# A hybrid decoder step on one core: a third buffer for the modulation blocks, six raw buffers instead of five for the experts

## The chip, the cores and the metric

The kernel runs on one core of one Trainium2 chip. The metric is the device time of one execution in microseconds (us), given as the median of several runs. Five engines run side by side, each with its own list of instructions, and wait for each other by semaphores: PE (TensorE, matmuls; PEld is its loading of weights, which overlaps PE), DVE (VectorE), ACT (ScalarE), POOL (GpSimd) and SP (SyncE, which here only issues transfers from HBM).

## The reference

One step of a decoder with two layers for 264 tokens (256 of a prompt, 8 that are decoded), width D = 1024, fp32:

```python
def _layer(x, c, l, p, st):
    mod = jax.nn.silu(c) @ p['w_ada'][l] + p['b_ada'][l]
    sh1, sc1, gt1, sh2, sc2, gt2 = [m[:, None, :] for m in jnp.split(mod, 6, axis=-1)]
    h = x * (1.0 + sc1) + sh1
    m, new_st = _mixer(h, l, p, st)
    x = _layernorm(ALPHA * x + (1.0 + gt1) * m, p['ln_mix_g'][l], p['ln_mix_b'][l])
    h = x * (1.0 + sc2) + sh2
    ...
    if l % 2 == 0:
        f = _swiglu(h, wg, wu, wd)            # layer 0, dense
    else:
        f = _moe(h, router, wg, wu, wd)       # layer 1, 2 of 8 experts
    return _layernorm(ALPHA * x + (1.0 + gt2) * f, p['ln_ffn_g'][l], p['ln_ffn_b'][l]), new_st
```

`_mixer` projects h once with `w_in`, runs three groups of heads on the parts (SSD, a chunked scan; RWKV-7, a recurrence for each token; GLA, a chunked scan), and projects their outputs with `w_out`. The modulation `mod` has 6 x 1024 columns a layer, so `w_ada` is 24 MB a layer, for 9 rows of c: much to load, little to multiply.

## The kernel before

Weights come as blocks of 128 x 1024 fp32 (512 KB). A block of `w_in`, `w_out`, of the dense feed-forward or of an expert goes through `block()`: SP loads it into a raw buffer `w` (L398), ACT copies it to a high part `wh` (L297), DVE subtracts to get a low part `wl` (L318), and PE multiplies it in three fp32r matmuls (hi x hi, hi x lo, lo x hi, L337). A raw buffer is free when DVE has made `wl`.

A block of `w_ada` goes through `ada()`. Its first blocks (tiles `k`, L474) are loaded at the start. The other 80 (tiles `wa`, L477) come in 20 steps of four, spread over both layers by a table (`FILL`) and where a value is needed (`need`). PE multiplies a `wa` block as it is, by the tile `sc` (silu of c): eight matmuls a block, 32 for a step, into the PSUM tile `ada`. A `wa` buffer is free when PE has done its eight matmuls. Then ACT copies `ada` (`adae`) and PE transposes it (`adat`).

Buffers stand in pools with a fixed number of slots. `self.wp` has `NW['w']` slots of 512 KB for raw `w` blocks, `self.ap` has `NW['a']` for `wa` blocks. An expert's block may be at home in either: the string `MOE['wa']` is gone through block by block, a letter for each, and "a" means `self.ap`. The small tiles of the mixers are in pools `f2` (of 128 x 2 x 264) and `f1` (of 128 x 264), numbered by `N2` and `N1`: pool 'r' holds the RWKV stream's tiles (and in the first stage the tiles `k`), pool 't' of `N1` small ones such as `w`, `ed`, `rs8`, `cslot`.

The order of the instructions on each engine is not written out: a list scheduler takes them by priority and by when a slot comes free, so that a changed number of slots also changes the order. All loads of weights and of the decoder's states stand on one queue, SP's, in one order: a load that waits for its slot holds up every load behind it.

```python
        spare = home == "a"
        w = (self.ap if spare else self.wp).tile([128, 1024], F32, tag="wa" if spare else "w", name=f"w_{self.n}")
        self.nc.sync.dma_start(w[:, :n], src)
        ...
                        w = self.ap.tile([128, 4, 256], F32, tag="wa", name=f"wa_{self.n}")
                        self.nc.sync.dma_start(w, src)
        ...
        homes = MOE["wa"]
        ...
            return self.block(self.I["moe"][e, m, b], by="wmoe", home=homes[self.blocks % len(homes)])
```

Names used below: `pj` is a matmul of the projection by `w_in` (from `hh`, `hl`, the two parts of h), `sro` and `gm` small matmuls of the decoder's RWKV read and of a norm, `mu` and `e` the sums of a norm, `gr` a product of the RWKV chunk's keys, `bk` and `sd` tiles that ACT makes for RWKV and for SSD (from `cu`, which is read back from HBM), `eg` the experts' gate and up products, `ed` their down products, `sc` the scattering of an expert's result to its tokens, `x` the residual that takes it, `xg` the gathering of an expert's tokens.

Of the kernel before, what the change touches and what calls it, by code (L numbers as in the profile page):

```python
# [166 lines left out]
def _unpack(r):  # L167
# [26 lines left out]
TP = {'a': 'ada adat st',  # L194
 'd': 'pj op eg0 ed eg1 ssq pos lg',
 'r': 'gr pa pb z p1 p2 p3 pn pr ph pg pc po gm gv gb gg1 ht cs sc gso fd gpo gpk lo gpv xg fg sro gvb pbt'}
N2 = {'r': 11, 'd': 16, 's': 14, 'g': 4, 'a': 1, 'q': 4, 'm': 3}
N1 = {'r': 10, 'd': 2, 's': 8, 't': 13, 'u': 6}
ORDER = [['rwkv', 'conv', 'rstep', 'qkv', 'aff', 'sstep', 'rout', 'gstep', 'gla', 'ssd', 'z2', 'gread', 'z1', 'z0'],
 ['rstep', 'rwkv', 'conv', 'sstep', 'qkv', 'rout', 'gstep', 'aff', 'gla', 'ssd', 'z0', 'z1', 'z2', 'gread']]  # L200
X = {'FR': 1, 'AHEAD': 1, 'SA': 4}
MOE = {'s0': 28, 'ss': 6, 'g0': 31, 'gs': 5, 'wa': 'wawaw', 'e0': 11, 'es': 5}
LOW = {'rout.0': -9440,
 'win.1': -20,
 'sstep.0': -1560,
# [44 lines left out]
 '1.o5': 1,  # L250
 '0.ssd': 1,
 '1.o6': 1}
NW = {'w': 3, 'a': 2, 'h': 3, 'l': 3}
NP = {'a': 1, 'd': 2, 'r': 3, 's': 2}


# [10 lines left out]
class Net:  # L267
    def __init__(self, nc, tc, I, O, stack):
        self.nc, self.tc, self.I, self.O = nc, tc, I, O
        p = lambda name, bufs, **k: stack.enter_context(tc.tile_pool(name=name, bufs=bufs, **k))  # L270
        self.cp = p("const", 1)
        self.wp = p("wts", NW["w"])
        self.ap = p("wada", NW["a"])
        self.hp = p("whi", NW["h"])
        self.lp = p("wlo", NW["l"])
        self.bp = p("big", 1)
        self.p2 = {t: p("f2" + t, n) for t, n in N2.items()}
        self.p1 = {t: p("f1" + t, n) for t, n in N1.items()}
        self.dp = p("scr", 1, space=bass.MemoryType.DRAM)
# [1297 lines left out]
    def experts(self, l, r, last, first=()):  # L1577

        nc, io = self.nc, self.C("iota")
        toks, mask, comb, pos, hth, htl = self.routed  # L1580
        homes = MOE["wa"]

# [10 lines left out]
        def gather(pr):  # L1593

            sel = []
            for t, (t0, n) in enumerate(toks):
                s = self.f1("sel", [128, 2, 128], F32R)
                if t == 2:
                    nc.gpsimd.memset(s.bitcast(F32), 0.0)
                for i in range(2):  # L1600
                    e = 2 * pr + i
                    chosen = self.ts(s[:n, i], io[:n], pos[:n, t, e:e + 1], OP.is_equal, mask[:n, t, e:e + 1], OP.mult)
                sel.append(s)
            yield
            name = "xg" if pr % 2 else "xo"
            xg = [[self.f2(name, [128, 2, 256], F32R) for _ in range(4)] for _ in range(2)]
            for k in range(8):
                for x, src in zip(xg, (hth, htl)):
                    ps = self.ps("xg", [128, 256])
                    for t, (t0, n) in enumerate(toks):  # L1610
                        self.mm(ps, src[t, k // 4][:, k % 4], sel[t].rearrange("p a b -> p (a b)"), t == 0, t == 2)
                    done = self.act(x[k // 2][:, k % 2], ps)
                yield
            self.affine((chosen, done))
            pc = self.ps("cs", [128, 2])
            cslot = self.f1("cslot", [128, 2])
            selt = []
            for i in range(2):
                e = 2 * pr + i
                for t, (t0, n) in enumerate(toks):  # L1620
                    self.mm(pc[:, i:i + 1], sel[t][:n, i].bitcast(F32), comb[:n, t, e:e + 1], t == 0, t == 2)
                ps = self.ps("st")[:, :TT]
                for t, (t0, n) in enumerate(toks):
                    self.tr(ps[:, t0:t0 + n], sel[t][:n, i].bitcast(F32))
                s = self.f1("selt", [128, TT], F32R)
                self.act(s, ps)
                selt.append(s)
            self.act(cslot, pc)
            G[pr] = xg, selt, cslot
            yield  # L1630
# [43 lines left out]
        def scatter(pr):  # L1674
            selt = G[pr][1]
            if last and pr == 3:
                V["st"] = self.stats()
            st = V["st"]
            self.need(l, 5)
            for d in range(8):  # L1680
                ps = self.ps("sc")[:, :TT]
                todo = [(y[:, d % 4], selt[i]) for i, yh, yl in Y[pr, d // 4] for y in (yh, yl)]
                for j, (y, s) in enumerate(todo):
                    self.mm(ps, y, s, j == 0, j == 3)
                self.residual(l, 5, d, ps, st, last=st is not None)
                yield
# [8 lines left out]
        for pr in range(4):  # L1695
            ahead = gather(pr + 1) if pr < 3 else iter(())
            V["at"], V["side"] = 0, [(MOE["s0"], MOE["ss"], back), (MOE["g0"], MOE["gs"], ahead)]
            if pr < 3:
# [4 lines left out]
            else:  # L1703
                for i in range(2):
                    up(pr, i)
                for n in range(2):
                    for i in range(2):
                        down(pr, i, n)
                    if n == 0:
                        for _ in back:  # L1710
                            pass
                        back = scatter(pr)
                        V["side"] = [(V["at"] + MOE["e0"], MOE["es"], back)]
                break
# [43 lines left out]
```

## Time and profile before

| | |
|---|---|
| median of 3 runs | 1104.17 us (1101.29 to 1107.13) |
| profiled execution | 1099.37 us, its span 1097.6 us |
| mean granted clock of TensorE | 0.966 |
| PE busy | 1006.8 us (92%) |
| DVE busy | 741.3 us (68%) |
| ACT busy | 609.6 us (56%) |
| moved by DMA | 238.55 MB, 217 GB/s in the mean |

The order of the stages in the profiled execution, by the timeline: the first modulation blocks and the projection of layer 0 up to some 81 us, the mixer of layer 0 to some 290, the dense feed-forward to some 493, the mixer of layer 1 to some 735, routing, the experts from 756 to 1080, and the end. The share of PE differs between them: in the feed-forward and in the experts it is nearly always busy, in the mixers not.

### The profile page before, as it was taken

How to read it: one execution, taken by the hardware profiler on the slowest of the kernel's cores; microseconds unless marked ns; L12 is line 12 of the kernel's file. 1: busy time of each engine (PE TensorE's matmuls, PEld its weight loads, DVE VectorE, ACT ScalarE, POOL GpSimd, SP SyncE). 2: the span in 40 equal slices, each digit the busy share in tenths (PEclk: the TensorE clock that was granted, in tenths of full speed). 3: DMA queues.
4: the chain of work that ended last, by engine and by line, in shares of the span. 5: the costliest groups of instructions: out<-in, count | busy, mean ns of one | idle time of the engine just before them, and what ended most of it. 6: DMA issues, size and time to landing. Idle time of an engine off the chain costs nothing. (4 is left out here: it accounts for less than half of the span.)

```text
span 1097.6 us, 22445 instructions
## 1 busy us (share of the span) xinstructions
PE 1006.8 (92%) x8944; PEld 825.8 (75%) x8944; DVE 741.3 (68%) x1406; ACT 609.6 (56%) x1037; POOL 87.6 (8%) x191
## 2 busy tenths in 40 slices
PE   6889987889899999998899998979999999999994
PEld 2668765557799999986677876757788888888872
DVE  1567647655765555448786686557879888888884
ACT  2656323543554444337671436438777777777773
POOL 1021222000100000001330220010000000000000
PEclk9999999999899999998989998989999999999998
DMA  9774478854565665555684284332998988898881
GB/s 353 279 216 130 141 206 305 269 179 137 176 207 175 183 181 173 146 162 192 196 253 143 81 275 163 103 101 77 328 323 299 329 321 299 308 327 299 318 299 42
DMA packets 71184, 238.55 MB, mean 217 GB/s; under 512 B 9280, under 2 KB 10016, under 8 KB 71072
## 3 DMA queue, kind: packets, MB, share of 16 engines
q1 hardware_dynamic: 66512, 226.18, 61.9%
q0 software_dynamic: 4000, 10.71, 3.5%
q8 instruction: 72, 1.18, 0.4%
q14 instruction: 40, 0.33, 0.1%
q10 hardware_dynamic: 560, 0.15, 0.1%
HBM read 231.50 MB, written 5.51 MB: 216 GB/s over the span
## 5 line engine op out<-in xcount | busy, mean ns | idle before, releaser
L318 DVE TENSOR_TENSOR wl<-w,wh 128x1024 fp32r<-128x1024 f32 (+1 forms) x324 | 390.1, 1216 | 130.0 <-ACT wh L297 125.8
L297 ACT ACTIVATE wh<-w 128x1024 fp32r<-128x1024 f32 (+1 forms) x324 | 338.4, 1053 | 237.6 <-issue 76.4
L337 PE MATMUL pj<-hh,wh 128*128 128x264 f32 x384 | 120.1, 315 | 6.7 <-ACT cv L297 2.8
L337 PE MATMUL pj<-hl,wh 128*128 128x264 f32 x384 | 120.1, 314 | 0.4 <-DVE hl L318 0.4
L337 PE MATMUL pj<-hh,wl 128*128 128x264 f32 x384 | 118.3, 309 | 1.1 <-DVE wl L318 1.1
L337 PEld LDWEIGHTS pj<-hh,wh 128*128 128x128 f32 x384 | 77.7, 203 | 15.7 <-issue 4.7
L337 PEld LDWEIGHTS pj<-hl,wh 128*128 128x128 f32 x384 | 77.3, 202 | 9.0 <-issue 6.5
L337 PEld LDWEIGHTS pj<-hh,wl 128*128 128x128 f32 x384 | 77.2, 202 | 7.6 <-issue 3.4
L337 PE MATMUL eg<-wh,xg 128*128 128x512 f32 x256 | 81.6, 397 | 0.0
L337 PE MATMUL eg<-wh,xo 128*128 128x512 f32 x256 | 81.5, 396 | 0.0
L337 PE MATMUL ada<-wa,sc 128*32 128x256 f32 x640 | 53.2, 415 | 25.4 <-DMA wa<-in_wada 20.9
L337 PEld LDWEIGHTS eg<-wh,xg 128*128 128x128 f32 x256 | 48.2, 188 | 9.5 <-ACT wh L297 0.3
L337 PEld LDWEIGHTS eg<-wh,xo 128*128 128x128 f32 x256 | 48.1, 188 | 9.2
L337 PE MATMUL eg<-wl,xg 128*128 128x512 f32 x128 | 51.6, 403 | 0.8 <-DVE wl L318 0.8
L337 PE MATMUL ed<-wl,ath 128*128 128x512 f32 x128 | 51.7, 404 | 0.6 <-DVE wl L318 0.6
L337 PE MATMUL eg<-wl,xo 128*128 128x512 f32 x128 | 51.4, 402 | 0.3 <-DVE wl L318 0.3
L337 PE MATMUL fg<-hh,wh 128*128 128x264 f32 x176 | 50.9, 289 | 0.0
L337 PE MATMUL ed<-wh,ath 128*128 128x512 f32 x128 | 50.8, 397 | 0.0
L337 PE MATMUL ed<-wh,atl 128*128 128x512 f32 x128 | 50.5, 395 | 0.0
L337 PE MATMUL fg<-hh,wl 128*128 128x264 f32 x176 | 50.4, 287 | 0.0
L337 PE MATMUL fu<-hh,wh 128*128 128x264 f32 x176 | 50.3, 286 | 0.0
L337 PE MATMUL fg<-hl,wh 128*128 128x264 f32 x176 | 50.2, 286 | 0.0
(486 smaller groups left out, 2282.6 us busy)
## 6 DMA issues: line engine op xcount, KB each, us to landing
w<-in_moe SPq DMA_DIRECT2D x192, 512.0 KB, 4.8
wa<-in_wada SPq DMA_DIRECT2D x80, 512.0 KB, 4.6
w<-in_win SPq DMA_DIRECT2D x48, 512.0 KB, 4.8
w<-in_ffgu SPq DMA_DIRECT2D x44, 512.0 KB, 3.6
k<-in_wada SPq DMA_DIRECT2D x32, 256.0 KB, 5.8
w<-in_wout SPq DMA_DIRECT2D x16, 512.0 KB, 4.5
w<-in_ffd SPq DMA_DIRECT2D x16, 512.0 KB, 3.5
w<-in_ffd SPq DMA_DIRECT2D x8, 384.0 KB, 3.9
```

What stands on the lines that cost most here:

```text
L297: r = self.nc.scalar.activation(out, in_, func, bias=bias, scale=scale)
L318: return (e or self.nc.vector).tensor_tensor(out, a, b, op=op)
L337: return self.nc.tensor.matmul(out, lhsT, rhs, start=start, stop=stop)
```

## The change

Four numbers and a string: `self.ap` gets three slots instead of two; the experts' blocks alternate between three `w` and three `wa` buffers, where before they took three of `w` and two of `wa` in a cycle of five; the pool of RWKV tiles of `f2` has 9 slots instead of 11, that of `f1` 7 instead of 10, and the pool of small tiles 10 instead of 13. The tables of priorities and of fillers stay.

```diff
-N2 = {'r': 11, 'd': 16, 's': 14, 'g': 4, 'a': 1, 'q': 4, 'm': 3}
-N1 = {'r': 10, 'd': 2, 's': 8, 't': 13, 'u': 6}
+N2 = {'r': 9, 'd': 16, 's': 14, 'g': 4, 'a': 1, 'q': 4, 'm': 3}
+N1 = {'r': 7, 'd': 2, 's': 8, 't': 10, 'u': 6}
...
-MOE = {'s0': 28, 'ss': 6, 'g0': 31, 'gs': 5, 'wa': 'wawaw', 'e0': 11, 'es': 5}
+MOE = {'s0': 28, 'ss': 6, 'g0': 31, 'gs': 5, 'wa': 'wa', 'e0': 11, 'es': 5}
...
-NW = {'w': 3, 'a': 2, 'h': 3, 'l': 3}
+NW = {'w': 3, 'a': 3, 'h': 3, 'l': 3}
```

The order of the instructions changes with it nearly everywhere in the mixers and in the experts. Three places follow; in them a number behind a name tells tiles of one name apart.

**PE, one modulation step in the mixer of layer 0** (step `ada_1995`, its four blocks `wa_1996`, `wa_2002`, `wa_2008` and `wa_2014`, with projection matmuls `pj` between). Before, the first two blocks stand together, and what follows up to the third is 20 rows of `sro`, `gm` and `pj`:

```order
L337 MATMUL pj_2068<-hh_347,wh_2064 128x264
L337 MATMUL ada_1995<-wa_1996,sc 32x256 x4
L337 MATMUL ada_1995<-wa_2002,sc 32x256 x4
L337 MATMUL sro_1912<-r_467,srw_1897 64x1 x16
L337 MATMUL pj_2068<-hl_348,wh_2064 128x264
L337 MATMUL pj_2068<-hh_347,wl_2065 128x264
L337 MATMUL pj_2068<-hh_347,wh_2064 128x264
L337 MATMUL gm_2267<-o_589,cst 128x264
```

In the changed kernel three blocks stand together, and the fourth comes after ten rows of `pj`:

```order
L337 MATMUL ada_1995<-wa_2002,sc 32x256 x4
L337 MATMUL ada_1995<-wa_2008,sc 32x256 x4
L337 MATMUL pj_2868<-hh_356,wl_2865 128x264
L337 MATMUL pj_2036<-hh_347,wl_2033 128x264
L337 MATMUL pj_2036<-hh_356,wh_2032 128x264
L337 MATMUL pj_2036<-hl_357,wh_2032 128x264
L337 MATMUL pj_2036<-hh_356,wl_2033 128x264
L337 MATMUL pj_2036<-hh_356,wh_2032 128x264
L337 MATMUL pj_2036<-hl_357,wh_2032 128x264
L337 MATMUL pj_2036<-hh_356,wl_2033 128x264
L337 MATMUL pj_2900<-hh_245,wh_2896 128x264
L337 MATMUL pj_2900<-hl_246,wh_2896 128x264
```

The row behind the last one shown is the block `wa_2014`. The third block moved up to the first two, into the new slot; the fourth is the one that waits for a slot of this step, that of `wa_1996`. Steps before a norm are the exception: there PE still has two blocks, the norm's `mu` and `e`, and two blocks.

**SP, the same stage** (`wa` are modulation blocks; `w_3060` is a block of `w_in`, `w_3143` and `w_3180` are blocks of `w_out`, `sgl` a state of the decoder). Before, loads of the two kinds take turns:

```order
L477 DMA wa_2107<-in_wada 128x1024
L477 DMA wa_2113<-in_wada 128x1024
L477 DMA wa_2129<-in_wada 128x1024
L398 DMA w_3060<-in_win 128x1024
L477 DMA wa_2135<-in_wada 128x1024
L398 DMA w_3143<-in_wout 128x1024
L477 DMA wa_2141<-in_wada 128x1024
L477 DMA wa_2147<-in_wada 128x1024
L1220 DMA sgl_2297<-in_s_gla 128x512
```

In the changed kernel the `wa` loads stand in a run, sixteen of them from `wa_2113` to `wa_2840` with the state `sgl` among them, and the `w` blocks come behind it:

```order
L477 DMA wa_2249<-in_wada 128x1024
L1220 DMA sgl_2297<-in_s_gla 128x512
L477 DMA wa_2701<-in_wada 128x1024
L477 DMA wa_2707<-in_wada 128x1024
L477 DMA wa_2713<-in_wada 128x1024
L477 DMA wa_2719<-in_wada 128x1024
L477 DMA wa_2828<-in_wada 128x1024
L477 DMA wa_2834<-in_wada 128x1024
L477 DMA wa_2840<-in_wada 128x1024
L398 DMA w_3060<-in_win 128x1024
L398 DMA w_3143<-in_wout 128x1024
```

So `w_3060` moved behind fourteen modulation blocks that it stood ahead of.

**PE, in the experts** (each scattering tile `sc` takes four matmuls, and each is followed by additions to `x` on DVE). Before, the four of one tile stand alone among the `eg` products:

```order
L337 MATMUL eg_1704_11751<-wh_11778,xg_11436 128x512
L337 MATMUL sc_12143<-selt_10896,eyh_11177 128x264
L337 MATMUL sc_12143<-selt_10896,eyl_11178 128x264
L337 MATMUL sc_12143<-selt_10905,eyh_11568 128x264
L337 MATMUL sc_12143<-selt_10905,eyl_11569 128x264
L337 MATMUL eg_1704_11751<-wl_11779,xg_11436 128x512
```

In the changed kernel four such tiles stand together behind the last product of an `eg` tile; the first ten rows of it:

```order
L337 MATMUL eg_1723_11910<-wh_11949,xg_11441 128x512
L337 MATMUL sc_12143<-selt_10896,eyh_11177 128x264
L337 MATMUL sc_12143<-selt_10896,eyl_11178 128x264
L337 MATMUL sc_12143<-selt_10905,eyh_11568 128x264
L337 MATMUL sc_12143<-selt_10905,eyl_11569 128x264
L337 MATMUL sc_12237<-selt_10896,eyh_11177 128x264
L337 MATMUL sc_12237<-selt_10896,eyl_11178 128x264
L337 MATMUL sc_12237<-selt_10905,eyh_11568 128x264
L337 MATMUL sc_12237<-selt_10905,eyl_11569 128x264
L337 MATMUL sc_12315<-selt_10896,eyh_11177 128x264
```

The scattering, gathering and sums beside the experts' products stand in 81 pieces instead of 117; nine of them instead of five have more than 0.9 us of PE work. On ACT, where `sd` stood ahead of `bk` in the mixer of layer 0, the first `bk` now stands ahead of `sd`, and the second `bk` and a tile `vt` behind it.

## Rows read from the trace of the kernel before

**Rows 1.** The page: the span, and the engines' busy time.

```profile
span 1097.6 us, 22445 instructions
...
PE 1006.8 (92%) x8944; PEld 825.8 (75%) x8944; DVE 741.3 (68%) x1406; ACT 609.6 (56%) x1037; POOL 87.6 (8%) x191
```

**Rows 2.** Busy time by stretch: the start, layer 0's mixer and its worst part, experts.

```profile
core 0: us, PE busy (x) PEld busy (x) DVE busy (x) ACT busy (x) POOL busy (x), PEclk, DMA share, GB/s
0.00:27.00 27.00, 17.10 (x116) 6.28 (x116) 4.66 (x13) 6.59 (x10) 4.08 (x18) 0.94 0.96 353
135.00:243.00 108.00, 88.21 (x1233) 62.77 (x1234) 64.28 (x157) 40.55 (x92) 16.06 (x27) 0.97 0.76 244
162.00:189.00 27.00, 20.18 (x163) 15.43 (x163) 18.60 (x40) 10.76 (x20) 4.30 (x8) 0.97 0.91 320
756.00:1080.00 324.00, 322.05 (x1563) 261.49 (x1562) 273.63 (x344) 242.08 (x306) 0.62 (x2) 1.00 0.85 299
```

**Rows 3.** Waits, whole span: engine, line, waited for, us, times, longest.

```profile
PEld ada L337 <- DMA wa<-in_wada: 26.3, 23, 3.8
PE ada L337 <- DMA wa<-in_wada: 20.9, 19, 3.6
```

**Rows 4.** The tile `wa`: its loads, and their time from issue to landing.

```profile
L477 SPq DMA_DIRECT2D wa<-in_wada x80: 327/328/839, 30.2 to 683.0; - x80
...
DMA to landing us min/median/max: 3.5/4.6/9.2
```

**Rows 5.** The wait of SP's queue ahead of `wa` loads.

```profile
SPq L477 <- PE ada L337: 116.7, 55, 18.4
```

**Rows 6.** Timeline of PE, 281 to 290 us: start, length, what, [idle before].

```profile
281.34 1.07 PE L337 MATMUL ada<-wa,sc 128*32 128x256 f32 x16
282.34 0.71 PE L337 MATMUL mu<-x,onem 128*128 128x264 f32 x2
282.89 0.62 PE L337 MATMUL e<-sq,onem 128*128 128x264 f32 x2
286.43 1.05 PE L337 MATMUL ada<-wa,sc 128*32 128x256 f32 x8 [2.92 <-DMA wa<-in_wada]
287.70 1.08 PE L337 MATMUL ada<-wa,sc 128*32 128x256 f32 x8 [0.22 <-DMA wa<-in_wada]
```

**Rows 7.** Timeline of SP's queue in the same stretch.

```profile
282.04 0.80 SPq L477 DMA_DIRECT2D wa<-in_wada  x2
```

**Rows 8.** Timeline of PE around 150 and around 186 us.

```profile
150.02 1.08 PE L337 MATMUL ada<-wa,sc 128*32 128x256 f32 x8 [3.57 <-DMA wa<-in_wada]
...
186.26 0.64 PE L337 MATMUL ada<-wa,sc 128*32 128x256 f32 x8 [2.86 <-DVE sst L318]
```

**Rows 9.** Stretches behind two waits for `wa`, columns as in Rows 2.

```profile
149.99:153.40 3.41, 3.38 (x19) 2.57 (x20) 1.50 (x3) 0.60 (x1) 0.56 (x1) 0.50 0.84 267
498.15:504.98 6.83, 6.20 (x35) 4.52 (x36) 6.79 (x21) 5.31 (x14) 2.94 (x9) 0.50 0.77 271
```

**Rows 10.** Timeline of PE, 76 to 84 us, in the mixer of layer 0.

```profile
81.08 0.45 PE L337 MATMUL gr<-sg,ka 64*64 64x64 f32 x12 [4.26 <-ACT bk L297]
```

**Rows 11.** Timeline of ACT in the same stretch.

```profile
78.13 1.27 ACT L297 ACTIVATE sd<-cu,tt 128x128 f32<-128x128 f32 x4 [5.38 <-DMA cu<-ssdd]
```

**Rows 12.** Waits within the experts, 756 to 1080 us.

```profile
ACT wh L297 <- DMA w<-in_moe: 15.5, 26, 1.8
...
PE eg L337 <- DVE wl L318: 1.1, 2, 0.8
...
PE ed L337 <- DVE wl L318: 0.6, 1, 0.6
```

**Rows 13.** Groups of instructions by form, 756 to 1080 us: count, busy, mean ns.

```profile
L318 DVE TENSOR_TENSOR wl<-w,wh 128x1024 fp32r<-128x1024 f32 x189 | 227.2, 1221 | 35.6 <-ACT wh L297 32.6 <-PE ed L337 1.0 <-PE eg L337 0.9
...
L297 ACT ACTIVATE wh<-w 128x1024 fp32r<-128x1024 f32 x189 | 197.3, 1057 | 40.7 <-DMA w<-in_moe 15.5 <-PE eg L337 12.9 <-PE ed L337 8.5
...
L334 DVE SCALAR_TENSOR_TENSOR x<-sc,mod,x 128x256 f32<-128x256 f32 x32 | 15.2, 475 | 0.0
```

## The prediction

> **What bounds the kernel now.** I read the page first, then busy time by stretch, then the waits, then timelines around single waits. The page shows PE busy for 1006.8 of 1097.6 us [rows 1]: 91 us in which it is not are all that better ordering can win. They are not spread evenly. In the experts PE works 322.05 of 324 us, at full clock [rows 2]; there only 2 us are left. In 135 to 243 us, the mixer of layer 0, it works 88.21 of 108 us, and its worst quarter, from 162 to 189, has 20.18 of 27. The list of waits names the largest single cause by PE's own matmuls: 20.9 us in 19 waits for a modulation block, 3.6 us at most [rows 3]. Weight loads wait 26.3 us for the same blocks; the two overlap, so I count the 20.9 and not the sum.
>
> Why is a block late? All 80 loads take 4.6 us from issue to landing at the median, 3.5 at least, 9.2 at most [rows 4]. SP waits 55 times for PE to free one of the two slots [rows 5]: it would load earlier if it could. The timeline at 281 us shows the pattern whole. PE runs two blocks in 1.07 us and has 1.3 us of other work; SP issues the next two at 282.04 when the first slot is free [rows 7], and PE takes the first of them at 286.43, after 2.92 us idle, and the second after 0.22 more [rows 6]. At 150.02 it waits 3.57 us; at 186.26 it waits 2.86 us, which the view puts down to DVE's `sst`, though these matmuls read only `wa` and `sc` [rows 8], so I count it to the block too.
>
> A wait also costs something behind it. From 149.99 the granted clock is 0.50 (1.2 GHz) for 3.41 us, and from 498.15 for 6.83 us, each right behind an idle PE [rows 9]. A stretch of 3.41 us at half clock does 1.7 us of full-speed work, so it costs about 1.7 us.
>
> **The third slot.** For each block I counted the PE work that stands between the block whose slot it takes and the block itself: each instruction in PE's order at the mean spacing that its tile shows in the trace of before, waits left out. A block then waits for what its landing exceeds that work. With a landing of 4.4 us, between the minimum and the median of [rows 4] and chosen because it fits, the two-slot order gives 21.6 us over 19 blocks, where the trace has 20.9 over 19 [rows 3]. That fit is one to the total, not to each block. The changed order with three slots gives 7.4 us over 9 blocks at the same landing. Gain: 14.2 us. At 3.5 us it is 10.2 against 3.3, gain 6.9; at 5.0 it is 35.4 against 15.6, gain 19.8.
>
> What remains follows from the order shown above. Three blocks of a step are now at hand, the fourth takes the slot of the first, and has two blocks and ten `pj` before it: at the spacings counted, about 3 us against 4.4. The steps in front of a norm hardly gain: with two blocks, `mu` and `e` between a slot's release and its next block there are 2.1 us of work, so about 2.3 us of the 2.92 + 0.22 of [rows 6] remain.
>
> **Loads that now go three at a time.** The count takes the same landing for all. Where three slots come free within some 1.1 us (the time of two blocks in [rows 6]) three loads share the transfer engines. At the 320 GB/s of 162 to 189 us [rows 2] 512 KB take 1.6 us, so the third may land up to 1.6 us later than the second. Below, this costs nothing: the third is often the one that is needed last. Above, I take a landing of 5.0 for the new order alone: 15.6 instead of 7.4 us, 8.2 more. I take 2, near the lower end, because the DMA share of the stage is 0.76 [rows 2], and a block loaded ahead of its need can land late for nothing.
>
> The Trainium skill's "DMA: Bandwidth & Descriptors", section "Issuing engines are not separate DMA queues", has the rule that speaks against the change: all transfers run on the same 16 engines and interleave. By it, one more transfer under way is no more bandwidth; taken alone it would put the slots and the clock at nothing and leave 1099.4 + 2 + 4.8 = 1106 us. The trace agrees in so far as the landings reach 9.2 us at a DMA share up to 0.91; it is the first two rivals below.
>
> **The clock.** The drops at 149.99 and behind 186.26 follow waits that the count removes: 2 x 1.7 = 3.4 us. Below, nothing, if a shorter wait there still brings one; above, also the two of 6.83 us behind 286.43 and 498.06, together 10.2 us. I take 3.4, since those two stand at norms, where the wait remains.
>
> **Six raw buffers for the experts.** ACT waits 15.5 us for their blocks, but PE only 1.1 + 0.6 us for what is made of them [rows 12]: the rest is covered by blocks already split. The gain lies between 0 and 1.7 us; I take 0.
>
> **The pieces between the experts' products.** Their PE work is the same. A tile `sc` brings two additions to `x` of 475 ns on DVE, where a `wl` takes 1.22 us [rows 13], and four tiles together hold DVE for some 3.8 us. DVE is busy 273.63 of 324 us [rows 2], so a late `wl` is caught up slowly. Before, five pieces above 0.9 us of PE work went with 1.7 us of PE waiting for `wl` in all [rows 12], 0.34 each. Nine would cost 3.1, or 1.4 more; at the worst each costs 1 us, 9 in all. I take 2, a little above the 1.4 for the busy DVE.
>
> **What else moves.** In the mixer PE waits 4.26 us at 81.08 for `bk` [rows 10], because `sd` ahead of it on ACT waits 5.38 us for `cu` [rows 11]. Now the first `bk` is ahead of `sd` and the second, with `vt`, behind it: PE goes on sooner and stops at the next tile instead. I take 0, with 4.3 us the other way as the bound of a gain, and as much of a loss if both stop. `w_3060`, now behind the run of modulation loads, has 8.9 us of counted PE work between its issue and its use, and needs about 4.6 [rows 4] + 1.06 + 1.22 us [rows 13] = 6.9. I take 0; if the run is issued 5 us late, it costs 3. Fewer slots in pool 'r': in the tiles' lifetimes I find nine of `f2` and seven of `f1` needed at once, so 0. The start, whose `k` tiles use these slots, is held by transfers (share 0.96 [rows 2]), so 0, 1 us at most.
>
> **Sum.** -14.2 - 3.4 + 2 + 2 = -13.6 us. From the profiled execution's 1099.4 that is 1085.8. The median of the runs shown is 4.8 us above that execution, so the forecast is 1091 us.
>
> **Rivals.**
> 1. *The transfers stretch.* If three in flight raise the mean landing of the new order to about 5.2 us, its sum (15.6 at 5.0, 37.4 at 6.0) comes to the 20.9 of now, and nothing is won: 1098 to 1107. For it: a share of 0.91 at 162 to 189 us, landings up to 9.2. Against it: the bytes are the same, and a quarter of the stage's transfer time is free.
> 2. *The same, further, and slower.* At a landing of 6.0 the new order waits 37.4 us, 16.5 more than now: 1104 + 16.5 = 1121. It ends above +0.5% from a landing of about 5.5 on (26.5 us). Its place is 135 to 243 us, where a run of `wa` loads competes with `w` and states. Against it: only the maximum landings are of that size now.
> 3. *The gain comes, and is given back.* PE waits for `w_3060` and the two `w_out` blocks behind it (3 us each, 9), or the experts' pieces cost 9 instead of 2. That leaves 1091 + 7 to 9 = about 1099, with both some 1107. For it: DVE at 84% in the experts. Against it: 322.05 of 324 us busy in spite of pieces of that size.
>
> **How the numbers follow.** What this kernel's measurement can tell from no change is about 0.5%, 5.5 us: 1098.7 to 1109.7. The forecast has 0.54 and a range of its own of 1083 to 1097 (counting at 5.0 in both orders, -19.8, or without the gain of the clock). Rival 1 has 0.15, rival 2 0.11, rival 3 0.20, half of it still below 1098.7. Faster: 0.54 + 0.10 + a little of rival 1 = 0.65; same: 0.22; slower: 0.13. The range that leaves out 2 in 10 is 1081 to 1106.
>
> **What would show it.** Right: PE's waits for `wa` at 7 to 11 us in some ten places, most of them for the fourth block of a step; PE busy for over 88% of the mixer of layer 0, where it is 82% now [rows 2]; granted clock full at 150 and 187; the experts' stretch within 3 us of now. Landing at 4.4 to 5.0 at the median. Wrong by rivals 1 and 2: a median landing above 5.2 and waits of 20 us or more. Wrong by rival 3: new PE waits for DVE `wl`, under `pj` and `op` in the mixer, or under `eg` and `ed` in the experts.

## The result, and the profile after

The changed kernel has a median of 1087.66 us (1085.42 to 1093.90, 4 runs) where the kernel before, beside it, has 1104.14 (1101.29 to 1107.13, 4 runs): a ratio of 0.9876, 95% interval 0.9846 to 0.9906. The forecast was 1091 us, with 1081 to 1106. A second comparison, with more runs on another occasion (run 5 below), gives 1093.57 against 1104.28: 0.9889, 0.9857 to 0.9921. That ratio leaves out three of the changed kernel's twelve executions, those more than 1.5% above its fastest; with all twelve the medians stand at 0.9903. So the change brings some 11 to 16 us. Between the two profiled executions the difference is 12.0 us: the changed kernel's has a span of 1085.6 us, that of [rows 1] 1097.6.

The page of the changed kernel, the span and the engines' busy time:

```profile
span 1085.6 us, 22435 instructions
...
PE 1009.1 (93%) x8944; PEld 825.7 (76%) x8944; DVE 744.1 (69%) x1406; ACT 610.3 (56%) x1037; POOL 85.3 (8%) x191
```

PE's busy time hardly moved; what fell is the time in which it waits. The waits of the whole span that answer to [rows 3] (engine, line, what for, total, times, longest), and with them the wait for the modulation step before, which [rows 3] did not need:

```profile
PEld ada L337 <- DMA wa<-in_wada: 13.9, 10, 2.9
PE ada L337 <- DMA wa<-in_wada: 11.1, 10, 2.4
...
PEld ada L337 <- DVE mod L493: 6.2, 7, 2.7
PE ada L337 <- DVE mod L493: 4.8, 4, 2.5
```

The last of them reads, in the kernel before:

```profile
PE ada L337 <- DVE mod L493: 1.2, 3, 0.4
```

From 20.9 us in 19 waits to 11.1 in 10: half of the places are gone. All ten that are left stand ahead of the fourth block of a step, as the prediction said of most of them; before, eight stood ahead of the third and nine ahead of the fourth. In exchange `ada` now waits for `mod`, 4.8 us instead of 1.2: a step's blocks are at hand, but the one PSUM tile that `ada` shares with `adat` still holds the step before, until DVE has read it. The queue that answers to [rows 5], and the landings that answer to [rows 4]:

```profile
SPq L477 <- PE ada L337: 83.6, 39, 9.4
```

```profile
DMA to landing us min/median/max: 3.4/5.1/9.8
```

Loads wait for PE 39 times, not 55. They take longer, 5.1 us at the median instead of 4.6. Yet the ten blocks that PE waited for landed after 4.7 us in the mean (counted as in the view, one by one: 3.7, 4.2, 6.5, 5.1, 5.7, 5.3, 4.1, 4.4, 4.1, 4.1), the other seventy after 5.6. Before it was the other way round: 5.6 us for the nineteen, 4.8 for the others. The long landings now fall on blocks that were loaded ahead of their need.

Busy time by stretch, layer 0's mixer (as in [rows 2]) and a part of it:

```profile
135.00:243.00 108.00, 95.71 (x1248) 66.10 (x1247) 68.90 (x166) 46.15 (x101) 13.05 (x22) 0.92 0.81 269
188.33:201.98 13.65, 13.55 (x244) 7.86 (x245) 5.33 (x21) 2.55 (x6) 0.00 (x0) 0.50 0.73 218
```

PE is busy for 95.71 of 108 us where it was 88.21, at a higher DMA share. But the granted clock of the row is 0.92 where [rows 2] has 0.97, so some 5 of the 7.5 us (0.05 of 108) can be the same work done more slowly, and the prediction's sign of over 88% is met in part by that. The second row is what was not expected: 13.65 us at half clock with PE busy nearly throughout. Three single waits on the timeline of PE:

```profile
173.42 0.64 PE L337 MATMUL ada<-wa,sc 128*32 128x256 f32 x8 [1.49 <-DVE mod L493]
...
188.43 1.08 PE L337 MATMUL ada<-wa,sc 128*32 128x256 f32 x8 [1.60 <-DMA wa<-in_wada]
```

```profile
278.11 0.64 PE L337 MATMUL ada<-wa,sc 128*32 128x256 f32 x8 [2.11 <-DMA wa<-in_wada]
```

The first is the new wait; the second ends where the half clock begins; the third is the fourth block at the norm, which had 2.92 + 0.22 us in [rows 6].

In the experts the time was not won. Stage lengths, read from the first or last row of a tile on PE's timeline (in brackets the time of it at granted clock 0.50):

| kernel (profiled execution) | 81 us to first `fg` | last `fd` to first `lg` | first `eg` to last `ed` | last `ed` to first `cnt` |
|---|---|---|---|---|
| before | 209.3 (17.4) | 243.0 (33.0) | 318.1 (0) | 11.1 (0) |
| changed | 199.2 (17.1) | 237.6 (27.5) | 317.1 (0) | 15.2 (0) |
| run 1, smaller pools alone | 208.2 (20.5) | 245.9 (36.2) | 318.1 (0) | 11.1 (0) |
| run 2, three slots, old cycle | 204.4 (23.5) | 239.1 (29.3) | 325.7 (0) | 15.2 (0) |
| run 3, scattering earlier | 199.2 (13.7) | 235.0 (18.2) | 323.6 (0) | 10.1 (0) |
| run 4, four slots | 202.4 (31.5) | 243.8 (36.0) | 318.7 (0) | 15.2 (0) |
| run 5, the change again (a long execution, 1101.8 us) | 208.6 (31.1) | 241.2 (35.2) | 317.3 (0) | 15.2 (0) |
| run 6, sums in a row | 195.9 (10.2) | 232.6 (21.4) | 317.8 (0) | 11.0 (0) |
| run 7, four slots, sums in a row | 199.1 (35.3) | 232.5 (11.7) | 319.4 (0) | 11.0 (0) |
| run 8, before with sums in a row | 205.4 (20.1) | 239.4 (31.3) | 320.6 (0) | 9.4 (0) |
| run 11, run 7 again | 195.8 (27.6) | 238.0 (34.2) | 319.4 (0) | 11.0 (0) |

In the first two rows the mixers gave 10.1 and 5.4 us, the experts' products 1.0; the tail behind the last product took 4.1 back. The lengths of the mixers hold the clock of their execution: in run 5 the same kernel has 66.3 us of them at half clock and hardly shorter mixers than before. With half of the time at half clock taken off, both mixers together are 427.1 and 425.8 us with two slots (before, run 1) and 414.5 and 416.6 with the change (changed, run 5), so 9 to 13 us shorter. In the tail PE is not idle. Its timeline in the kernel before, from the last product on:

```profile
1073.08 0.40 PE L337 MATMUL ed<-wh,atl 128*128 128x512 f32 x1
1073.41 0.41 PE L337 MATMUL ms<-x,onem 128*32 128x264 f32 x1
1073.42 0.41 PE L337 MATMUL ms<-sq,onem 128*32 128x264 f32 x1
1073.42 0.41 PE L337 MATMUL ms<-x,onem 128*32 128x264 f32 x1
1073.43 0.41 PE L337 MATMUL ms<-sq,onem 128*32 128x264 f32 x1
...
1074.12 0.39 PE L337 MATMUL ms<-x,onem 128*32 128x264 f32 x1
1074.43 0.39 PE L337 MATMUL sc<-selt,eyh 128*128 128x264 f32 x1
```

and in the changed kernel:

```profile
1057.26 0.40 PE L337 MATMUL ed<-wh,atl 128*128 128x512 f32 x1
1057.49 0.28 PE L337 MATMUL sc<-selt,eyl 128*128 128x264 f32 x1
...
1058.96 0.28 PE L337 MATMUL sc<-selt,eyl 128*128 128x264 f32 x1
1059.29 0.63 PE L337 MATMUL ms<-x,onem 128*32 128x264 f32 x2
1059.75 0.63 PE L337 MATMUL ms<-sq,onem 128*32 128x264 f32 x2
```

`ms` are the sums of the last norm, in four groups of 32 columns. Before, the products of four groups start within 0.02 us of each other, and 14 recorded rows take 1.1 us. Now they come mostly one group at a time, in pieces between `sc` rows: four rows take 1.1 us. Also 29 `sc` rows stand behind the last `ed` and not 16; the other thirteen stood between the products before, so their time, some 1.6 us, only changed its place.

### The profile page after: what moved, and what is told of

It reads as the page before. It is cut to its first block, busy times and chain, and to the rows that moved or that the text cites. A ratio compares the mean times of both kernels' runs of the same rounds, so it can differ in the third digit from the quotient of the medians.

```text
span 1085.6 us, 22435 instructions
## 1 busy us (share of the span) xinstructions
PE 1009.1 (93%) x8944; PEld 825.7 (76%) x8944; DVE 744.1 (69%) x1406; ACT 610.3 (56%) x1037; POOL 85.3 (8%) x191
## 5 line engine op out<-in xcount | busy, mean ns | idle before, releaser
L337 PE MATMUL pj<-hl,wh 128*128 128x264 f32 x384 | 116.4, 304 | 0.2 <-DVE hl L318 0.2
L337 PEld LDWEIGHTS pj<-hh,wl 128*128 128x128 f32 x384 | 76.8, 200 | 10.1 <-issue 6.8
L337 PE MATMUL ada<-wa,sc 128*32 128x256 f32 x640 | 50.9, 412 | 15.1 <-DMA wa<-in_wada 11.1
L337 PE MATMUL fu<-hl,wh 128*128 128x264 f32 x176 | 50.5, 287 | 0.0
```

The lines of the kernel that those rows point to most:

```text
L337: return self.nc.tensor.matmul(out, lhsT, rhs, start=start, stop=stop)
```

## The experiments

All are timed beside the kernel before. "Changed" is the kernel of this study; where a run starts from it, the diff is against it.

**1. The smaller pools alone** (from changed: the third slot and the cycle taken back).

```diff
-MOE = {..., 'wa': 'wa', 'e0': 11, 'es': 5}
+MOE = {..., 'wa': 'wawaw', 'e0': 11, 'es': 5}
-NW = {'w': 3, 'a': 3, 'h': 3, 'l': 3}
+NW = {'w': 3, 'a': 2, 'h': 3, 'l': 3}
```

> The smaller pools of RWKV tiles and small tiles alone, with two buffers for modulation blocks and the experts' five raw buffers as before. The order of every engine is then that of the kernel before, row for row; only addresses move. My theory (the cut slots were never needed together): no change, 1104 us within 3, waits of PE for modulation blocks about 21 us again. Rival (the cut slots cost something that the third buffer hid): 2 us or more above the kernel before.

1104.56 us, ratio 1.0013 (0.9979 to 1.0046). Block waits:

```profile
PE ada L337 <- DMA wa<-in_wada: 23.5, 21, 3.1
```

The cut slots cost nothing, as the prediction had it.

**2. Three slots, the experts' old cycle** (from changed).

```diff
-MOE = {..., 'wa': 'wa', 'e0': 11, 'es': 5}
+MOE = {..., 'wa': 'wawaw', 'e0': 11, 'es': 5}
```

> The changed kernel with the experts' cycle of three w and two wa letters put back (so the third wa buffer is there, and the experts still use all six buffers, in another cycle). My theory (the gain is the modulation blocks'): as the changed kernel, 1088 us within 2, PE's waits for modulation blocks about 11 us, and the stretch from the first eg product to the end as long as in the changed kernel, 332 us, with some 29 scattering matmuls behind the last ed product. Rival (the even cycle of the experts' buffers carries part of the gain, or made the end longer): 3 us or more of difference, in the experts' stretch.

1103.42 us, ratio 1.0016 (0.9978 to 1.0054): the theory missed, and the rival came. Block waits are down as they should be (11.9 us in 10), and the mixers are shorter. But the experts' products take 325.7 us instead of 317.1. Waits of this kernel from 748 to 1074 us:

```profile
ACT wh L297 <- DMA w<-in_moe: 14.2, 27, 2.4
PEld eg L337 <- DVE wl L318: 8.9, 17, 1.1
...
PE eg L337 <- DVE wl L318: 3.6, 8, 0.8
```

and of the changed kernel from 740 to 1058, where no wait of ACT for an expert's block is listed:

```profile
PEld ed L337 <- DVE wl L318: 1.1, 4, 0.3
...
PEld eg L337 <- DVE wl L318: 0.7, 3, 0.3
```

In the kernel before, from 756 to 1080 us, the second line is

```profile
PEld eg L337 <- DVE wl L318: 3.7, 10, 1.1
```

With three slots the scheduler orders the experts as it does in the changed kernel (81 pieces of side work). In the old cycle a `w` buffer comes round after five blocks, in the even cycle over six buffers after six. ACT's wait for raw blocks is no longer here than in the kernel before (15.5 us, [rows 12]), but what follows from it reaches PE: its loading of weights waits 8.9 us for `wl`, with the old order 3.7, with the even cycle 0.7. That the new order, with fewer and larger pieces between the products, leaves less of a reserve of split blocks would fit this; it is not shown by itself.

**3. The last scattering earlier** (from changed).

```diff
-MOE = {..., 'wa': 'wa', 'e0': 11, 'es': 5}
+MOE = {..., 'wa': 'wa', 'e0': 0, 'es': 2}
```

> The changed kernel, with the last pair's first four scattering tiles put between its last four ed blocks in the program (the start of the side work 0 and its step 2 instead of 11 and 5), so that 16 instead of 29 scattering matmuls stand behind the last ed product. Theory: the experts gave back 3 us in the tail behind the last product (10.8 us instead of 6.7 in the kernel before), not in the larger pieces of side work; the tail falls to 6 to 7.5 us and the time by 3 to 4, to 1084. Rival (the pieces cost it, between the products): the tail shortens but the products end as much later, or nothing changes: 1087 to 1089.

1095.46 us, 0.9938 (0.9903 to 0.9972), no gain over the changed kernel. The tail fell from 15.2 to 10.1 us, but the products take 6.5 longer: the rival, though its 1087 to 1089 us were too low as well. `sc` and single `ms` rows now stand between `ed` rows and cost PE the same there. So it is their spacing on PE, not where they stand, that must be paid for; run 6 follows from it.

**4. Four slots** (from changed).

```diff
-NW = {'w': 3, 'a': 3, 'h': 3, 'l': 3}
+NW = {'w': 3, 'a': 4, 'h': 3, 'l': 3}
```

> The changed kernel with a fourth buffer for modulation blocks. My theory (a wait is the landing less the work between a slot's release and its use): the count at a landing of 4.4 gives 0.1 us instead of 7.4, at 5.0 it is 0.8 instead of 15.6, so PE's waits for modulation blocks fall from 11 us to under 3, and the time by 5 to 10, to 1078 to 1083; what is left before a step's first block is the wait for the step before it (one PSUM tile), 4 to 7 us. Rival (transfers bind: four in flight only land later): landings above 6 us at the median, waits of 8 us or more, 1086 to 1092.

1095.97 us, 0.9936 (0.9903 to 0.9968). Its waits, its landings, and a stretch of the mixer:

```profile
PE ada L337 <- DVE mod L493: 5.1, 3, 4.3
...
PE ada L337 <- DVE mod L318: 2.3, 1, 2.3
...
PE ada L337 <- DMA wa<-in_wada: 1.8, 3, 0.9
```

```profile
DMA to landing us min/median/max: 3.4/6.1/12.1
```

```profile
190.47:214.36 23.89, 22.72 (x398) 15.00 (x398) 10.01 (x36) 10.78 (x30) 0.57 (x1) 0.50 0.67 215
```

The count was about right (0.1 to 0.8 us counted, 1.8 measured), at a landing of 6.1 us, so transfers do not bind. The time did not follow: 31.5 and 36.0 us of the two mixers are at half clock, against 17.1 and 27.5, and `mod` is waited for. The mean granted clock over the runs is 0.959, against 0.966 for the changed kernel in run 5. So taking 9 us more of block waits away brought no time in the median.

**5. The change again**, unaltered.

> The changed kernel once more, unaltered, beside the kernel before on one chip in many runs. Three slots, four slots and two slots have shown, in single profiles corrected by half of the time at half clock, 712, 707 and 722 us up to the experts' first product. Theory (the third slot is worth about 10 us ahead of the experts, the experts give back 3): 7 to 9 us below the kernel before at equal granted clock, so 1093 to 1096 where that has 1102.6; PE's waits for modulation blocks 11 to 13 us; experts from the first eg product to the end 332 us. Rival (the gain of 16 us of the first comparison is of the change alone): 1086 to 1088.

1093.57 us, 0.9889 (0.9857 to 0.9921): as expected, and with the first comparison's interval overlapping. In its profile the block waits are 9.9 us in 9 places, a little below what was expected, and the wait for `mod` is 8.5 us in 4. The mean granted clock is 0.966 over 12 runs, for the kernel before 0.960 over 17. At a span near 1100 us the time that the clock takes is at most span x (1 - clock), 37 against 44 us. So up to some 6 of the 10.7 us are the clock's.

**6. The norms' sums in a row** (from changed; in all four norms).

```diff
-                for i, a in zip((0, 64, 32, 96), st["todo"]):
-                    self.mm(st["ms"][i:i + 32, :TT], self.onem[:, :32], a, start=d == 1, stop=d == 5)
+                last = None
+                for i, a in list(zip((0, 64, 32, 96), st["todo"]))[::-1]:
+                    self.tc.cur_priority -= 10 ** 5 if last else 0
+                    r = self.mm(st["ms"][i:i + 32, :TT], self.onem[:, :32], a, start=d == 1, stop=d == 5)
+                    self.tc.cur_priority += 10 ** 5 if last else 0
+                    if last:
+                        self.order(r, last)
+                    last = r
```

> The changed kernel, with the four small products of a norm's sums (tile ms, four column groups of 32) kept next to each other on PE in all four norms. Theory: the tail behind the last ed product is 4 us longer than in the kernel before (10.8 against 6.6) because its 24 recorded ms rows alternate with scattering rows and take 0.25 us each, where the kernel before has 14 of them in a row in 1.1 us. In a row, the tail falls by 2 to 4 us, to 7 to 9, the time by as much against the changed kernel in the same call, a little more if the other norms gain too. Rival (the tail is set by the additions to x on DVE or by the number of scattering rows, 29 instead of 16): the tail stays at 10 to 11.

1077.51 us, 0.9767 (0.9727 to 0.9808), some 13 us (by the ratios) to 16 us (by the medians) below the changed kernel of run 5, where 2 to 4 and a little more were expected. One group of sums in its tail:

```profile
1050.64 0.41 PE L337 MATMUL ms<-sq,onem 128*32 128x264 f32 x1
1050.65 0.41 PE L337 MATMUL ms<-x,onem 128*32 128x264 f32 x1
1050.65 0.41 PE L337 MATMUL ms<-sq,onem 128*32 128x264 f32 x1
1050.66 0.41 PE L337 MATMUL ms<-x,onem 128*32 128x264 f32 x1
```

The tail is 11.0 us, 4.2 less than changed. Over all four norms the spacing of the `ms` rows, from each to the next on PE with waits left out, sums to 7.1 us; it is 17.5 in the kernel before and 21.3 in the changed one. So the change had also cost 3.8 us of PE here, 2.1 in the tail (5.6 against 3.5) and 1.7 at the norm behind layer 0's mixer (5.5 against 3.8), and 14.2 were to be had: the other three norms gain more than the tail that the run was meant for.

**7. Four slots and sums in a row** (run 4's edit on run 6).

> The kernel of the sums in a row with a fourth buffer for modulation blocks. Theory (waits for blocks and the tail add up): 4 to 6 us below the changed kernel at equal granted clock; if the granted clock falls as it did with four slots alone (0.959 in the mean against 0.965 with three), that takes back some 6 us and the two are equal, 1091 to 1096. Rival (the lower clock with four slots was chance): 1086 to 1090.

1074.24 us, 0.9740 (0.9704 to 0.9776), far below both forecasts, since the sums in a row bring more than they counted. The mean clock of its runs is 0.964, so four slots need not bring the low clock of run 4. That the edit adds to run 6 is not settled: the intervals overlap.

**8. The kernel before with its sums in a row** (run 6's edit on the kernel before).

> The kernel before (two slots, five raw buffers, large pools), with the norms' sums kept in a row as in the run of the changed kernel. It gives the worth of the third slot without the tail. Theory (third slot: 10 us of block waits and some 4 us of granted clock, tail 4 us against it): the sums in a row give the kernel before some 10 us (their spacing sums to 17.5 us, in a row to 7.1), so 1092 to 1095, ratio 0.989 to 0.992, with block waits of 21 to 24 us as before; the third slot is then worth 14 to 18 us between this and the changed kernel with the same edit (1077.5), more than the 10.7 of the unaltered pair. Rival (the third slot's worth is some 7 to 10 us, and the sums interplay with it elsewhere): this kernel at 1084 to 1088.

1089.33 us, 0.9860 (0.9819 to 0.9902), between the theory's and the rival's range; block waits 20.9 us in 18. Against run 6 the third slot, the cycle and the pools are worth 0.9860 - 0.9767 = 0.0093, about 10 us, with an interval of some 6 us either way, about as much as in the unaltered pair: the theory's 14 to 18 missed. Its tail is 9.4 us (run 6: 11.0, with thirteen `sc` rows more), but its products take 320.6 us (run 6: 317.8), so in the experts the two end up nearly level, and the theory, which had counted the whole 4 us of the tail for the third slot, counted too much.

**9. The transposed modulation in another PSUM pool** (from run 7).

```diff
- TP = {'a': 'ada adat st',
+ TP = {'a': 'ada st',
-  'r': 'gr pa pb z ... gvb pbt'}
+  'r': 'gr pa pb z ... gvb pbt adat'}
```

> Four slots, sums in a row, and the transposed modulation (adat) in the pool of three PSUM tiles of the RWKV stream instead of the one tile that it shares with ada. Theory: with four slots PE no longer waits for blocks but for the step before (16 us of idle time ahead of ada that the view puts to DVE mod); in another bank that wait goes, but the steps stand closer and blocks are late again: the count at a landing of 4.4 gives 11.6 us where it gave 0.1. So mod waits fall below 5 us, block waits rise to 8 to 15, and the time stays within 4 us of the same kernel with the shared tile, 1074. Rival (the shared tile is the bound): 6 us or more below, 1068 or less.

1102.51 us, 0.9992 (0.9961 to 1.0022): 28 us worse than run 7, the farthest miss. The waits of `ada` moved as expected, no wait for `mod` and

```profile
PE ada L337 <- DMA wa<-in_wada: 11.9, 10, 5.7
```

but the clock did not stay:

```profile
177.33:194.40 17.07, 9.59 (x57) 3.16 (x57) 6.19 (x21) 1.92 (x4) 0.55 (x1) 0.50 0.83 295
...
228.53:238.77 10.24, 10.24 (x51) 7.73 (x50) 5.54 (x12) 2.60 (x9) 0.82 (x2) 0.50 0.18 65
```

Its profile has 51.2 us at half clock in layer 0's mixer and 47.7 in layer 1's (run 7: 35.3 and 11.7), the mean over its runs is 0.949. In the first row PE is idle for 7.5 us; in the second not at all. Against the 0.964 of run 7 that clock takes at most some 18 of the 28 us. The rest is not accounted for: in place of 9.0 us of PE's waits for `mod` in run 7 stand 11 us more of block waits, and that RWKV's own products now share their three PSUM tiles with `adat` is a rival that was not tested.

**10. The even cycle alone** (from the kernel before, two slots).

```diff
-MOE = {..., 'wa': 'wawaw', 'e0': 11, 'es': 5}
+MOE = {..., 'wa': 'wa', 'e0': 11, 'es': 5}
```

> The kernel before with only the experts' cycle changed to one w, one wa, over three w and two wa buffers (five, not six). With the kernel before, the changed one and the one of three slots and the old cycle it closes the square of the two parts. A wa buffer then comes round after four blocks. PE takes 318 us for 192 blocks, 1.66 us each, so four are 6.6 us; landing 4.8, ACT 1.06 and DVE 1.22 together are 7.1. Theory (the cycle must fit the number of buffers; the gain of the change needs both parts): the experts' products take 10 to 25 us longer than the 318 of now, the time is 1110 to 1125; block waits in the mixers stay at 21 to 24 us. Rival (the even cycle is better in itself, whatever the number): 1100 or less.

1127.56 us, 1.0227 (1.0196 to 1.0258), a little above what was expected, with block waits of 25.8 us. Its products take 339.0 us from 769.1 on, within what was expected. Waits from 769 to 1108 us:

```profile
ACT wh L297 <- DMA w<-in_moe: 68.0, 69, 2.1
...
PEld eg L337 <- ACT wh L297: 10.1, 21, 0.8
PEld eg L337 <- DVE wl L318: 8.5, 14, 1.1
```

The square of the two parts is closed: two slots and the old cycle 318.1 us of products, even cycle alone 339.0, third slot alone 325.7, both 317.1. Either part alone loses in the experts; only together they don't.

**11. Run 7 again.**

> Four slots and the sums in a row once more, the fastest version so far, in a second comparison. Expected: ratio to the kernel before 0.972 to 0.977; block waits of PE below 2 us; the stretch from the first eg product to the end 330 us. If the first comparison was a lucky one: 0.980 or more.

1078.70 us, 0.9782 (0.9752 to 0.9811), just above what was expected. Block waits are 4.3 us and not below 2, the mean clock of its runs is 0.961. Runs 6, 7 and 11 are the fastest versions, 23 to 30 us below the kernel before; which of three and four slots is better stays open.

## Why the prediction was right, point by point

**The third slot** was the main term and its mechanism held: a block waits for what its landing exceeds the work between its slot's release and itself. The count gave 21.6, 7.4 and 0.1 us for two, three and four slots, the profiles have 20.9 to 23.5 (before, runs 1 and 8), 9.9 to 13.8 (changed, runs 2, 3, 5 and 6), and 0.9 to 4.3 (runs 4, 7 and 11). With the 2 us for loads that go three at a time it said 9.4 for three; 11.1 was measured, a gain of 9.8 by the view of waits where -12.2 stood in the sum. The wait at 186.26, which the prediction had put to a block but not into its 20.9, is gone as well (2.9 us). Against that stands a wait that the count could not see, the one for `mod`: 3.6 us more than before, in run 5 7.3.

**The landing.** Rival 1 put its turning point at 5.2 us and the median did come to 5.1, in four-slot kernels to 6.1 to 6.3, and still the waits fell. The rival failed because it let every landing grow alike. In the changed kernel longer landings belong to blocks with time to spare (5.6 us in the mean); the ones that PE waited for took 4.7.

**The clock** was right in sign over many runs (0.966 against 0.960, up to some 6 us) and wrong in its working. The drop at 149.99 is gone. The one behind 186.26 came back at 188.33 and lasted 13.65 us, and a new one of 3.41 us stands at 167.85. In the two profiles the time at half clock in both mixers is 50.4 us before and 44.6 after, so 2.9 us of work where 3.4 was forecast; that this comes so near is luck, since other single profiles have 56.7 (run 1, the old order) and 66.3 (run 5, the change again). That removing a wait removes the stretch behind it is not so: it can come back at the next wait, and longer.

**Six raw buffers** stood at 0, and measured against the kernel before that is what the products show: they are 1.0 us shorter, with thirteen `sc` rows (1.6 us) less between them. But the reason given, that PE hardly waits for raw blocks, was that of the old order. With the new order they are what keeps the products at 317 us and not 326 (run 2). Without this part of the change nothing would have been won (1103.42 us). The prediction treated two parts as a sum that are not one; that its 0 held was luck.

**The pieces** stood at +2, and the experts did take 3.1 us more (332.3 against 329.2 from the first `eg` to `cnt`). The size was near and the reason and place were wrong: no wait of PE for `wl` is left between the products, and with the thirteen `sc` rows counted they grew by no more than some 0.6 us. The loss is in the tail, 2.1 us of it from sums that alternate with scattering rows. This is shown by the timelines and by run 6, where the sums alone were moved and the tail fell by 4.2 (1.7 of it the kernel before can gain too, run 8).

**The rest** held: the smaller pools cost nothing (run 1), `w_3060` brought no new wait of PE for a `w_in` block, the stall at 81.08 turned into one of 2.72 us at 80.52 (in run 5 of 4.35 at 81.67), within the bounds of 4.3 either way. Rivals 2 and 3 did not come. One bound of the prediction does not follow from its terms: without the gain of the clock its sum is -10.2, so 1094 us and not the 1097 of its inner range.

So the sum of -13.6 met -12.0 in the profiles and -10.7 to -16.5 in the medians, and that it is so near is in part luck: the terms that were off had both signs. What makes the two comparisons differ by 6 us is not settled; the mean clock of the changed kernel's runs was 0.969 in the first and 0.966 in the second.

## What to carry to other kernels

Count, from the trace of before and the order of both kernels, the work between the release of a slot and the use of the block that takes it, for each block: a total that fits the waits of now gave the waits of one slot and of two slots more. It gives waits and not time: the fourth slot took 9 us of waits away, and the median time did not fall (run 4). Where buffers are shared by a cycle, the cycle, the number of buffers and the order must fit each other; run each part alone before crediting the whole. When PE is "busy" in a tail, look at the spacing of its rows: small products in different column groups belong next to each other.

## What the runs showed of the hardware that was not expected

Four products for 32 columns each, in four column groups, overlap when they stand in a row: 14 rows in 1.1 us, 0.08 each. Between other products two rows take some 0.6 us. Keeping them in a row in all four norms gave 13 to 16 us of 1094.

A stretch at half clock can far outlast the wait that it follows, with PE busy all through it: 13.65 us with 13.55 busy, 23.89 with 22.72, 10.24 with 10.24. In the first of these PE ran five modulation blocks, products of GLA (`gg`) and some fifteen recorded `pj`. In the kernel before, the same part of the mixer, with more `pj` between, stayed at full clock in spite of 4.5 us idle:

```profile
190.95:216.00 25.05, 20.57 (x535) 15.04 (x535) 17.63 (x60) 11.20 (x23) 2.15 (x4) 1.00 0.82 252
```

What sets the length of such a stretch was not tried. Shorter waits for blocks did not go with a higher clock: 0.959 in the mean with 1.8 us of them (run 4), 0.966 with 9.9 (run 5).
